# Softmax sums applied to the attention's values through diagonal tiles, in a hybrid encoder block on one core

## The chip, the core and the metric

The kernel runs on one core of one Trainium2 chip. The metric is the device time of one execution in microseconds (us). The engines are named as the profile names them: PE (TensorE, matrix products and transposes), PEld (its weight loads, which overlap its products), DVE (VectorE), ACT (ScalarE), POOL (GpSimd) and SP (SyncE, which here issues most of the DMAs). Each engine works through its own queue in order, and semaphores make it wait for the others.

## The reference

One encoder layer over 1024 tokens of width 1024, in float32. A combined projection of the normalised input feeds two groups of heads: attention in a window, with 8 query heads that share 2 key and value heads of width 64, and a gated DeltaNet (GDN) of 4 heads in both directions. Their outputs are concatenated, projected by W_out and added to the input; a feed-forward network with squared ReLU and a last normalisation follow. The change lies in the attention, for a block of 128 queries against a band of up to three blocks of keys:

```python
scores = jnp.einsum("bnqkgd,bnskd->bnkgqs", qb, kb).astype(jnp.float32) * (ATTN_HEAD_DIM ** -0.5)
scores = scores + bias
scores = jnp.where(valid, scores, -1e30)
probs = jax.nn.softmax(jnp.concatenate([scores, sink_col], axis=-1), axis=-1)[..., :-1]
out = jnp.einsum("bnkgqs,bnskd->bnqkgd", probs.astype(v.dtype), vb)
```

The softmax has one more column, a learned sink for each head, which enters its sum and has no value. So each query's output is a sum of values weighted by exponentials, divided by one number for each query and head.

## The kernel before, in words

The layer runs in stages: the norm and the transposes of the input, the projections, the preparation of the GDN (triangular inversions), the attention and the two scans of the GDN, the output projection, then the feed-forward network as products of a fast block scheme. The large products are made of three matmuls with operands split into a high and a low part (L124, L125, L126; L119 makes the high part on ACT, L120 the low part on POOL).

From about 335 to 590 us of the span two streams of work are woven together by weights: generators yield an estimate of the work that they issued, and the weaver takes the stream that is furthest behind. One stream is `output()`: the attention, then the attention's half of the output projection (`out_attn`), then the GDN's half (`out_all`, which calls `out_gdn` for each block of 128 tokens) with the tokens of the second half of the feed-forward input (`tokens_second`). The other has the last inversions and the scans forward and backward. This gives the order in which the program is written; a scheduler that runs over it then sets each engine's order.

The attention goes over 8 blocks of queries n and the 2 key heads kv. `attn_scores` makes the scores of 4 query heads (two matmuls each, L544 and L545), adds the bias and takes the maximum on DVE (L546), exponentiates on ACT with the sum as an accumulated output (L558), adds the sink's part to the sum and takes the reciprocal on DVE (L559, L560), and then multiplies the probabilities of each head by it, three heads on DVE and one on POOL (all recorded at L563). Three steps later `attn_transpose` turns the probabilities on PE (L573, four transposes for each block of keys) and ACT copies them out of PSUM (L575). When both key heads are there, `attn_value` multiplies them with the values (L585: for each block of keys a pair of matmuls, one for each key head, with 64 columns of weights each, so that the output has the two key heads in the two halves of the partitions and 4 heads x 128 queries in its columns); DVE copies the result (L588), and SP stores it (L589) in a buffer in HBM, `mad`. `query` loads the next queries by a DMA that POOL issues (L594).

`out_attn` loads a block of `mad` back (L885), splits it (L119, L120) and projects it, with DVE adding to the residual stream (L876). `out_gdn` sums squares on ACT (L900), makes the norm's factor in small operations on DVE (L902 to L905) and POOL (L906), multiplies by it on DVE (L907), transposes on PE (L910) and multiplies by the gate on DVE (L911). `tokens_second` transposes the normalised rows (L209), scales them on ACT (L966, L214), makes the low parts and differences on DVE (L215, L970), and splits the differences (L949 on ACT, L950 on DVE or POOL). The scans' matmuls are L797, and their steps on DVE L810, L815, L816, L825, L836 and L843. The inversions are the lines L720 to L764.

Matmul results lie in two rings of 4 PSUM buffers: `psA` (scores, transposed probabilities, values, output projection) and `psB` (scans, tokens). In SBUF there are rings of equal buffers, among them `pg` (28), `sc` (4), `wr` (4) and `pt` (12).

Of the kernel before, what the change touches and what calls it, by code (L numbers as in the profile page):

```python
# [16 lines left out]
P = 128  # L17
# [60 lines left out]
class Block:  # L78
# [198 lines left out]
    def proj_ab(self, raw):  # L277
# [5 lines left out]
        nc.vector.tensor_copy(out=whz[:, :, 0:16], in_=whl[:, :, 0:16].bitcast(F32))  # L283
        zero = self.small((P, NK * 16), bufs=1, tag="zab")
        nc.gpsimd.memset(zero, 0.0)
# [11 lines left out]
        for c in range(NT):  # L297
            nc.tensor.transpose(ps[:, c, :], ab[:, c * P:(c + 1) * P], self.ident[0:32, 0:32])
        abt = self.small((P, NT, 32), bufs=1, tag="abt")
        nc.vector.tensor_copy(out=abt, in_=ps)  # L300
# [3 lines left out]
    def gates(self, ps):  # L304
# [3 lines left out]
        mk = lambda name: c.tile([P, NT, 8], F32, name=name)  # L308
        tmp = lambda: self.small((P, NT, 8), bufs=6, tag="gt")
        vt = nc.vector  # L310
# [29 lines left out]
        nc.tensor.matmul(gps[:, 1], self.ones, g, start=True, stop=True)  # L340
        gc2 = self.small((P, NT, 8), bufs=1, tag="gc2")
        self.ngc, self.egc, self.negc, self.egl, self.ew = (mk(n) for n in ("ngc", "egc", "negc", "egl", "ew"))
# [10 lines left out]
        rr = self.sc((64, 2, P))  # L353
        part = self.small((64, 3, P), bufs=1, tag="gparts", dt=BF16)
        nc.scalar.copy(out=part[:, 0, :], in_=tp)
# [176 lines left out]
    def attn_scores(self, n, kv, mx, q, mk):  # L532
# [4 lines left out]
        for gp in range(2):  # L537
# [12 lines left out]
            tiles.append(s)  # L550
        nm, es, sm = (self.small((P, 4), tag="nm", bufs=12) for _ in range(3))
        ns = self.nsink[:, 4 * kv:4 * kv + 4]
# [7 lines left out]
        nc.vector.reciprocal(out=sm, in_=sm)  # L560
        for g in range(4):
            s = tiles[g // 2][:, g % 2, :width]
            (nc.gpsimd if g == 3 else nc.vector).tensor_scalar(out=s, in0=s, scalar1=sm[:, g:g + 1], scalar2=None,  # L563
                                                               op0=ALU.mult)
        return tiles, list(range(lo, hi))

# [11 lines left out]

    def attn_value(self, n, pts, kbs):
        nc = self.nc  # L580
        ps = self.ps("psA")
        last = len(kbs) - 1
        for j in range(last, -1, -1):
            for kv in (1, 0):
                nc.tensor.matmul(ps[64 * kv:64 * kv + 64, :], self.va[:, kbs[j], 64 * kv:64 * kv + 64],  # L585
                                 pts[kv][j].rearrange("p g q -> p (g q)"), start=j == last, stop=j == 0)
        o = self.pt()
        nc.vector.tensor_copy(out=o, in_=ps)  # L588
        nc.sync.dma_start(out=self.mad[n], in_=o)  # L589
# [7 lines left out]
    def attention(self):  # L597

        steps = [(n, kv) for n in range(NT) for kv in range(2)]
        qs = self.qs  # L600
        open_, pts = [], []

        def close():
            n, kv, tiles, kbs = open_.pop(0)
            pts.append(self.attn_transpose(tiles, kbs))
            yield 1.3
            if kv == 1:
                self.attn_value(n, pts[:], kbs)
                pts.clear()
                yield 2.6  # L610

        for i, (n, kv) in enumerate(steps):
            mk = self.pg if i % 3 == 2 else self.wr
            open_.append((n, kv, *self.attn_scores(n, kv, self.small((P, 4), tag="nm", bufs=12), qs.pop(0), mk)))
            if i + 2 < len(steps):
                qs.append(self.query(*steps[i + 2]))
            yield 1.3
            if len(open_) > 2:
                yield from close()
        while open_:  # L620
            yield from close()
# [756 lines left out]
```

## Time and profile before

| what | value |
|---|---|
| time, three runs | 1256.77, 1258.15, 1258.52 us; median 1258.15 |
| span of the profiled execution | 1253.3 us |
| its own time | not given |
| mean granted clock of TensorE | 0.983 |
| PE, PEld busy | 95%, 77% of the span |
| DVE, ACT, POOL busy | 68%, 50%, 46% |

The span goes from the first to the last instruction of one profiled execution; the time of a run has what lies around it too. A group's line in the profile gives the line of the code, the engine, the operation, output and inputs with their sizes, how many there were, the busy time of all and the mean of one in ns, and behind the second bar the engine's idle time just ahead of them with what ended it. An f32 matmul is recorded as two instructions. The ends of matmuls are modelled, so the busy time of PE says that it had work, not that it ran at its peak.

### The profile page before, as it was taken

How to read it: one execution, taken by the hardware profiler on the slowest of the kernel's cores; microseconds unless marked ns; L12 is line 12 of the kernel's file. 1: busy time of each engine (PE TensorE's matmuls, PEld its weight loads, DVE VectorE, ACT ScalarE, POOL GpSimd, SP SyncE). 2: the span in 40 equal slices, each digit the busy share in tenths (PEclk: the TensorE clock that was granted, in tenths of full speed). 3: DMA queues.
4: the chain of work that ended last, by engine and by line, in shares of the span. 5: the costliest groups of instructions: out<-in, count | busy, mean ns of one | idle time of the engine just before them, and what ended most of it. 6: DMA issues, size and time to landing. Idle time of an engine off the chain costs nothing.

```text
span 1253.3 us, 18527 instructions
## 1 busy us (share of the span) xinstructions
PE 1191.6 (95%) x6482; PEld 967.2 (77%) x6482; DVE 854.9 (68%) x1528; ACT 621.4 (50%) x1347; POOL 580.3 (46%) x488
## 2 busy tenths in 40 slices
PE   7999999899789989998999999999999999999997
PEld 5778777677568868877788888888777888888885
DVE  5667667982389986676655454544668797886976
ACT  6455688335485752125464554545545434444343
POOL 5354211362432433144573534535445665655595
PEclk9999999899889999998999999999999999999999
DMA  7134344441956678122234344443678624434323
GB/s 239 52 121 133 101 171 140 139 126 40 223 168 158 190 216 296 60 84 85 84 131 159 132 151 143 154 159 134 223 280 280 223 85 167 151 121 148 95 90 135
DMA packets 121630, 187.62 MB, mean 150 GB/s; under 512 B 11043, under 2 KB 64416, under 8 KB 121537
## 3 DMA queue, kind: packets, MB, share of 16 engines
q1 hardware_dynamic: 96708, 152.58, 37.9%
q10 hardware_dynamic: 16381, 29.67, 6.3%
q0 software_dynamic: 8448, 4.20, 1.9%
q8 instruction: 51, 0.84, 0.3%
q14 instruction: 42, 0.34, 0.1%
HBM read 122.39 MB, written 63.49 MB: 148 GB/s over the span
## 4 chain that ended last, share of the span: by engine, by line
PE 49%; DVE 6%; DMA 3%; issue 2%; POOL 1%; ACT 1%; ACTq 0%; POOLq 0%; DVEq 0%; SPq 0%
PE psA L124 8%; PE psA L125 8%; PE psA L126 8%; PE psB L126 7%; PE psB L125 7%; PE psB L124 7%; DMA pg<-sd 3%; PE psB L797 2%; DVE pg L1154 1%; DVE pt L1163 1%; DVE wr L1166 1%; PE psB L209 1%; DVE pg L1199 1%; DMA sd<-pt 0%; DVE wr L1161 0%
## 5 line engine op out<-in xcount | busy, mean ns | idle before, releaser
L124 PE MATMUL psA<-pg,wh 128*128 128x512 f32 x416 | 167.6, 404 | 2.1 <-ACT pt L458 2.1
L126 PE MATMUL psA<-pg,wl 128*128 128x512 f32 x416 | 166.9, 401 | 0.0
L125 PE MATMUL psA<-pg,wh 128*128 128x512 f32 x416 | 166.5, 400 | 0.0
L120 POOL TENSOR_TENSOR wl<-wr,wh 128x512 fp32r<-128x512 f32 x44 | 70.2, 1618 | 154.0 <-ACT wh L119 153.9
L1154 DVE TENSOR_TENSOR pg<-pg 128x512 fp32r<-128x512 f32 x112 | 122.7, 1127 | 18.8 <-ACT pg L1153 18.6
L120 POOL TENSOR_TENSOR wh<-wr,wh 128x512 fp32r<-128x512 f32 x32 | 47.9, 1518 | 131.5 <-ACT wh L119 131.5
L1071 ACT ACTIVATE pt<-pt 128x512 f32<-128x512 f32 x64 | 40.4, 632 | 122.7 <-DVE pt L1061 122.7
L125 PE MATMUL psA<-pg,pg 128*128 128x512 f32 x256 | 99.7, 391 | 0.5 <-POOL pg L120 0.5
L124 PE MATMUL psA<-pg,pg 128*128 128x512 f32 x256 | 99.0, 391 | 1.0 <-DVE pg L1199 1.0
L126 PE MATMUL psA<-pg,pg 128*128 128x512 f32 x256 | 99.7, 389 | 0.0
L120 POOL TENSOR_TENSOR pg<-wr,pg 128x512 fp32r<-128x512 f32 x48 | 73.4, 1560 | 51.0 <-ACT pg L119 51.0
L124 PEld LDWEIGHTS psA<-pg,wh 128*128 128x128 f32 x416 | 79.2, 190 | 21.3 <-ACT pt L458 2.4
L125 PEld LDWEIGHTS psA<-pg,wh 128*128 128x128 f32 x416 | 79.3, 191 | 19.7 <-issue 0.9
L126 PEld LDWEIGHTS psA<-pg,wl 128*128 128x128 f32 x416 | 79.1, 190 | 18.6
L1153 ACT CAST pg<-pg 128x512 fp32r<-128x512 f32 x112 | 67.2, 620 | 41.3 <-DMA pg<-sd 31.0
L126 PE MATMUL psB<-pg,pg 128*128 128x512 f32 x192 | 75.0, 390 | 1.3 <-DVE pg L1154 1.3
L125 PE MATMUL psB<-pg,pg 128*128 128x512 f32 x192 | 75.0, 391 | 0.8 <-POOL pg L120 0.7
L124 PE MATMUL psB<-pg,pg 128*128 128x512 f32 x192 | 74.7, 390 | 0.4 <-ACT pg L1153 0.4
L119 ACT CAST wh<-wr 128x512 fp32r<-128x512 f32 x76 | 43.6, 623 | 45.5 <-PE psA L125 24.8
L1061 DVE TENSOR_TENSOR pt<-psB,pt 128x512 f32<-128x512 f32 x39 | 26.9, 689 | 55.1 <-PE psB L126 30.1
L1061 DVE TENSOR_TENSOR pt<-psA,pt 128x512 f32<-128x512 f32 x39 | 26.8, 689 | 55.0 <-PE psA L126 39.5
L124 PEld LDWEIGHTS psA<-pg,pg 128*128 128x128 f32 x256 | 48.0, 188 | 12.6 <-DVE pg L1199 2.3
(385 smaller groups left out, 3307.7 us busy)
## 6 DMA issues: line engine op xcount, KB each, us to landing
sd<-pt ACTq DMA_DIRECT2D x112, 256.0 KB, 2.2
pg<-sd SPq DMA_DIRECT2D x112, 256.0 KB, 2.9
wr<-in_w_ffn_in SPq DMA_DIRECT2D x32, 512.0 KB, 3.8
wr<-in_w_in SPq DMA_DIRECT2D x22, 512.0 KB, 4.8
pg<-in_x SPq DMA_DIRECT2D x16, 512.0 KB, 5.4
wr<-in_w_ffn_out SPq DMA_DIRECT2D x16, 512.0 KB, 4.8
sc<-kvd SPq DMA_DIRECT2D x14, 512.0 KB, 4.1
kvd<-pt SPq DMA_DIRECT2D x16, 256.0 KB, 2.8
```

Source lines behind the costliest of these rows:

```text
L119: nc.scalar.copy(out=h, in_=raw)
L120: (eng or nc.gpsimd).tensor_tensor(out=l, in0=raw, in1=h.bitcast(F32), op=ALU.subtract)
L124: nc.tensor.matmul(ps, wh, xh, start=first, stop=False, skip_group_check=onto)
L125: nc.tensor.matmul(ps, wh, xl, start=False, stop=False, skip_group_check=onto)
L126: nc.tensor.matmul(ps, wl, xh, start=False, stop=last, skip_group_check=onto)
L209: self.nc.tensor.transpose(ps[:, i * P:(i + 1) * P], row[:, k * P:(k + 1) * P], self.ident)
L797: nc.tensor.matmul(ps[:, h - g.start, :], left(h), right[:, h, :], start=True, stop=True)
L1061: self.nc.vector.tensor_tensor(out=out, in0=in0, in1=in1, op=ALU.add)
L1071: self.nc.scalar.activation(out=c, in_=c, func=AF.Relu)
L1153: nc.scalar.copy(out=s[:, 0], in_=raw)
L1154: v.tensor_tensor(out=s[:, 1], in0=raw, in1=s[:, 0].bitcast(F32), op=ALU.subtract)
L1163: v.tensor_tensor(out=b["T2"], in0=b["B22"], in1=b["T1"], op=ALU.subtract)
```

## The change

The multiplication of the probabilities is taken out. `attn_scores` now returns the reciprocals of the sums as well, 128 queries x 4 heads. For each of the 16 pairs of query block and key head, POOL multiplies the identity by them (`diagonal`, recorded at the line after L567): a tile of four 128x128 diagonals. `attn_value` first multiplies a matrix of ones with 64 columns by each key head's diagonals: the sum over the partitions leaves one row with the reciprocal of each query and head, the same in all 64 output partitions, as the values' output has them. ACT copies that out of PSUM into the second diagonal's tile, and DVE multiplies the values by it where it copied them before.

```diff
-        for g in range(4):
-            s = tiles[g // 2][:, g % 2, :width]
-            (nc.gpsimd if g == 3 else nc.vector).tensor_scalar(out=s, in0=s, scalar1=sm[:, g:g + 1], scalar2=None,
-                                                               op0=ALU.mult)
-        return tiles, list(range(lo, hi))
+        return tiles, list(range(lo, hi)), sm
+
+    def diagonal(self, r):
+
+        dg = self.buf("dg", 2, (P, 4, P))
+        self.nc.gpsimd.tensor_tensor(out=dg, in0=self.ident.unsqueeze(1).to_broadcast([P, 4, P]),
+                                     in1=r.unsqueeze(2).to_broadcast([P, 4, P]), op=ALU.mult)
+        return dg
...
-    def attn_value(self, n, pts, kbs):
-        nc = self.nc
+    def attn_value(self, n, pts, kbs, dgs):
+
+        nc = self.nc
+        rec = self.ps("psA")
+        for kv in (1, 0):
+            nc.tensor.matmul(rec[64 * kv:64 * kv + 64, :], self.ones[:, 64 * kv:64 * kv + 64],
+                             dgs[kv].rearrange("p g q -> p (g q)"), start=True, stop=True)
+        scale = dgs[1].rearrange("p g q -> p (g q)")
+        nc.scalar.copy(out=scale, in_=rec)
         ps = self.ps("psA")
...
         o = self.pt()
-        nc.vector.tensor_copy(out=o, in_=ps)
+        nc.vector.tensor_tensor(out=o, in0=ps, in1=scale, op=ALU.mult)
         nc.sync.dma_start(out=self.mad[n], in_=o)
...
-            n, kv, tiles, kbs = open_.pop(0)
+            n, kv, tiles, kbs, r = open_.pop(0)
+            dgs.append(self.diagonal(r))
             pts.append(self.attn_transpose(tiles, kbs))
             yield 1.3
             if kv == 1:
-                self.attn_value(n, pts[:], kbs)
+                self.attn_value(n, pts[:], kbs, dgs[:])
                 pts.clear()
-                yield 2.6
+                dgs.clear()
+                yield 3.0
```

Besides, the ring of the small tiles of `attn_scores` grows from 12 to 16, and some small temporaries at the start of the kernel (L284, L299, L309, L341, L354) move into `pt` buffers, which makes room for the two diagonal tiles. In the lines of the changed kernel, L546 and L547 are the score matmuls, L578 the transposes of the probabilities, L580 their copy, L589 the new matmuls, L592 the new copy, L597 the value matmuls, L600 the new product, L811 the scans' matmuls; L876, L907, L910, L911, L950 and L970 have become L890, L921, L924, L925, L964 and L984.

The change moves instructions as well. On PE, in the middle of the attention before: the transposes of a block's probabilities, scan matmuls, then the value matmuls (an operand's number tells buffers apart, `x2` is two matmuls in a row).

```order
L573 MATMUL psA_4399<-ident,wr_4132 128x128 x2
L573 MATMUL psA_4399<-ident,wr_4141 128x128 x2
L797 MATMUL psB_4406<-sc_4324,sc_4323 128x128 x2
L797 MATMUL psB_4411<-sc_4324,sc_4323 128x128 x2
L797 MATMUL psB_4416<-sc_4198,pg_4319 128x128 x2
L797 MATMUL psB_4421<-sc_4324,pt_4326 128x128 x2
L585 MATMUL psA_4434<-pt_4404,pg_2381 64x512
L585 MATMUL psA_4434<-pt_4316,pg_2381 64x512
```

The same place on PE after:

```order
L578 MATMUL psA_4408<-ident,wr_4115 128x128 x2
L578 MATMUL psA_4408<-ident,wr_4124 128x128 x2
L811 MATMUL psB_4364<-sc_4284,sc_4283 128x128 x2
L811 MATMUL psB_4369<-sc_4284,sc_4283 128x128 x2
L811 MATMUL psB_4374<-sc_4156,pg_4279 128x128 x2
L589 MATMUL psA_4415<-dg_4392,ones 64x512
L589 MATMUL psA_4415<-dg_4308,ones 64x512
L811 MATMUL psB_4379<-sc_4284,pt_4286 128x128 x2
L597 MATMUL psA_4419<-pt_4413,pg_2374 64x512
L597 MATMUL psA_4419<-pt_4329,pg_2374 64x512
```

The new pair stands between the block's transposes and its value matmuls, here with scan matmuls on both sides; that is so for seven of the eight blocks.

At the end of the attention on PE, between the last value matmul and the first matmul of the output projection (L124), before:

```order
L585 MATMUL psA_4927<-pt_4888,pg_2381 64x512
L797 MATMUL psB_4919<-sc_4869,pt_4871 128x128 x2
L797 MATMUL psB_4923<-sc_4869,pt_4871 128x128 x2
L797 MATMUL psB_4947<-sc_4869,pg_4621 128x128 x2
...
L797 MATMUL psB_5050<-sc_4943,pg_4318 128x128 x2
L797 MATMUL psB_5055<-sc_4943,pg_4318 128x128 x2
L124 MATMUL psA_4975<-pg_4746,pt_4969 128x512
```

The same place on PE after:

```order
L597 MATMUL psA_4952<-pt_4891,pg_2374 64x512
L811 MATMUL psB_4975<-sc_4924,pt_4926 128x128 x2
L811 MATMUL psB_4979<-sc_4840,pg_4547 128x128 x2
L811 MATMUL psB_4984<-sc_4924,pt_4926 128x128 x2
...
L811 MATMUL psB_5068<-sc_5025,sc_5024 128x128 x2
L811 MATMUL psB_5073<-sc_4924,pg_4279 128x128 x2
L124 MATMUL psA_4996<-pg_4675,pt_4990 128x512
```

Before, 14 such rows, 28 scan matmuls, stand between the two; after, 10 rows, 20 matmuls.

On DVE, where the last `out_gdn` meets `tokens_second`, before:

```order
L215 SCALAR_TENSOR_TENSOR pg_6097<-psB_6092,cols,pg_6097 128x512
L905 TENSOR_TENSOR sm_5997<-sm_5997,sq_1234 128x4
L970 SCALAR_TENSOR_TENSOR pg_6085<-psB_6092,cols,pg_6085 128x512
L215 SCALAR_TENSOR_TENSOR pg_6136<-psB_6131,cols,pg_6136 128x512
L970 SCALAR_TENSOR_TENSOR pg_6124<-psB_6131,cols,pg_6124 128x512
L907 TENSOR_TENSOR wr_5995<-pg_3794,sm_5998 128x512
L950 TENSOR_TENSOR pg_6140<-pg_6085,pg_6140 128x512
L215 SCALAR_TENSOR_TENSOR pg_6169<-psB_6164,cols,pg_6169 128x512
L970 SCALAR_TENSOR_TENSOR pg_6143<-psB_6164,cols,pg_6143 128x512
L911 SCALAR_TENSOR_TENSOR wr_5994<-psA_6010,cols,wr_5995 128x512
```

The same place on DVE after:

```order
L984 SCALAR_TENSOR_TENSOR pg_6117<-psB_6124,cols,pg_6117 128x512
L917 TENSOR_SCALAR sm_5990<-sm_5990 128x4
L964 TENSOR_TENSOR pg_6133<-pg_6078,pg_6133 128x512
L918 RECIPROCAL sm_5990<-sm_5990 128x4
L215 SCALAR_TENSOR_TENSOR pg_6162<-psB_6157,cols,pg_6162 128x512
L984 SCALAR_TENSOR_TENSOR pg_6136<-psB_6157,cols,pg_6136 128x512
L919 TENSOR_TENSOR sm_5990<-sm_5990,sq_1227 128x4
L215 SCALAR_TENSOR_TENSOR pg_6190<-psB_6185,cols,pg_6190 128x512
L984 SCALAR_TENSOR_TENSOR pg_6169<-psB_6185,cols,pg_6169 128x512
L964 TENSOR_TENSOR pg_6194<-pg_6136,pg_6194 128x512
L921 TENSOR_TENSOR wr_5988<-pg_3775,sm_5991 128x512
L925 SCALAR_TENSOR_TENSOR wr_5987<-psA_6003,cols,wr_5988 128x512
```

The multiplication by the norm's factor (L907, now L921), which stood behind two of the four L215 and L970 pairs, stands behind all four and both L950 (L964). On PE the order there is as before: the 32 transposes of the tokens, the four transposes of this block (L910, now L924), the matmuls of the output projection.

More of the change, by code (lines that the diff above doesn't have):

```diff
@@ L283, in proj_ab @@
         nc.vector.tensor_copy(out=whz[:, :, 0:16], in_=whl[:, :, 0:16].bitcast(F32))
-        zero = self.small((P, NK * 16), bufs=1, tag="zab")
+        zero = self.pt((P, NK * 16))
         nc.gpsimd.memset(zero, 0.0)
@@ L298, in proj_ab @@
             nc.tensor.transpose(ps[:, c, :], ab[:, c * P:(c + 1) * P], self.ident[0:32, 0:32])
-        abt = self.small((P, NT, 32), bufs=1, tag="abt")
+        abt = self.pt((P, NT, 32))
         nc.vector.tensor_copy(out=abt, in_=ps)
@@ L308, in gates @@
         mk = lambda name: c.tile([P, NT, 8], F32, name=name)
-        tmp = lambda: self.small((P, NT, 8), bufs=6, tag="gt")
+        spare = self.pt((P, 8, NT, 8))
+        free = iter(range(8))
+        tmp = lambda: spare[:, next(free)]
         vt = nc.vector
@@ L340, in gates @@
         nc.tensor.matmul(gps[:, 1], self.ones, g, start=True, stop=True)
-        gc2 = self.small((P, NT, 8), bufs=1, tag="gc2")
+        gc2 = tmp()
         self.ngc, self.egc, self.negc, self.egl, self.ew = (mk(n) for n in ("ngc", "egc", "negc", "egl", "ew"))
@@ L353, in gates @@
         rr = self.sc((64, 2, P))
-        part = self.small((64, 3, P), bufs=1, tag="gparts", dt=BF16)
+        part = self.pt((64, 3, P), BF16)
         nc.scalar.copy(out=part[:, 0, :], in_=tp)
@@ L550, in attn_scores @@
             tiles.append(s)
-        nm, es, sm = (self.small((P, 4), tag="nm", bufs=12) for _ in range(3))
+        nm, es, sm = (self.small((P, 4), tag="nm", bufs=16) for _ in range(3))
         ns = self.nsink[:, 4 * kv:4 * kv + 4]
@@ L600, in attention @@
         qs = self.qs
-        open_, pts = [], []
+        open_, pts, dgs = [], [], []
         def close():
-            n, kv, tiles, kbs = open_.pop(0)
+            n, kv, tiles, kbs, r = open_.pop(0)
+            dgs.append(self.diagonal(r))
             pts.append(self.attn_transpose(tiles, kbs))
@@ L607, in close @@
             if kv == 1:
-                self.attn_value(n, pts[:], kbs)
+                self.attn_value(n, pts[:], kbs, dgs[:])
                 pts.clear()
-                yield 2.6
+                dgs.clear()
+                yield 3.0
         for i, (n, kv) in enumerate(steps):
             mk = self.pg if i % 3 == 2 else self.wr
-            open_.append((n, kv, *self.attn_scores(n, kv, self.small((P, 4), tag="nm", bufs=12), qs.pop(0), mk)))
+            open_.append((n, kv, *self.attn_scores(n, kv, self.small((P, 4), tag="nm", bufs=16), qs.pop(0), mk)))
             if i + 2 < len(steps):
```

## The prediction

> **What bounds the kernel now.** The first view is the page: the span and the busy time of each engine.
>
> ```profile
> span 1253.3 us, 18527 instructions
> PE 1191.6 (95%) x6482; PEld 967.2 (77%) x6482; DVE 854.9 (68%) x1528; ACT 621.4 (50%) x1347; POOL 580.3 (46%) x488
> ```
>
> PE is busy for 95% of the span, so as a whole the kernel is bound by TensorE. The change touches only the attention, so the second view cuts out its neighbourhood: the last inversion (335 to 365), the attention woven with the scans (to 475), the attention's half of the output projection woven with the last scan (to 530), and the end of that scan (to 545). The columns are the stretch, its length, the busy time of PE, of the weight loads (PEld), of DVE, ACT and POOL, then granted clock, DMA share and GB/s.
>
> ```profile
> 335.00:365.00 30.00, 23.21 (x451) 18.50 (x450) 21.73 (x70) 24.43 (x61) 14.45 (x18) 0.77 0.60 160
> 365.00:475.00 110.00, 101.53 (x771) 83.51 (x772) 101.32 (x337) 68.86 (x200) 35.06 (x31) 1.00 0.73 209
> 475.00:530.00 55.00, 55.00 (x305) 47.37 (x304) 32.84 (x90) 9.64 (x35) 15.17 (x13) 1.00 0.48 168
> 530.00:545.00 15.00, 12.15 (x71) 10.33 (x70) 13.89 (x34) 5.20 (x15) 8.46 (x6) 0.89 0.17 52
> ```
>
> The attention's stretch is the one place where two engines are near their limit together: PE 101.53 and DVE 101.32 of 110 us. Just behind it, from 475 on, PE has no idle time at all. Which of the two ends the other's waits is the third view, PE's waits from 335 to 475, with total, times and longest:
>
> ```profile
> PE psB L753 <- DVE pt L746: 3.1, 3, 2.2
> PE psB L720 <- DMA pg<-atd: 3.1, 2, 2.1
> PE psB L797 <- DVE sc L815: 2.8, 3, 1.2
> PE psA L573 <- DVE pt L588: 1.7, 1, 1.7
> PE psA L585 <- ACT pt L575: 1.6, 2, 0.9
> PE psA L544 <- DMA pt<-qad: 0.8, 1, 0.8
> PE psB L797 <- DVE sc L810: 0.6, 1, 0.6
> PE psB L761 <- ACT pt L755: 0.5, 1, 0.5
> PE psB L797 <- DVE sc L825: 0.5, 1, 0.5
> PE psA L544 <- DVE pt L588: 0.3, 1, 0.3
> ```
>
> They sum to 14.0 us: DVE ends 3.1 + 2.8 + 1.7 + 0.6 + 0.5 + 0.3 = 9.0, ACT 1.6 + 0.5 = 2.1, DMA 3.1 + 0.8 = 3.9. So in 140 us PE stands still for 14, and a lighter DVE can give back 9 of them at most. Against that, whatever is added to PE is paid in full, since PE works the rest of the time.
>
> **Removed: the 64 multiplications of the probabilities.** The groups of their line, from 335 to 475, with the busy time of DVE and of POOL:
>
> ```profile
> 335.00:475.00 140.00, 24.43 (x48) 20.93 (x16) 0.95 0.70 198
> ```
>
> DVE loses 24.43 us in 48 instructions, POOL 20.93 in 16. DVE is not on the end's path by itself; what comes back is a share of the 9.0 us. I estimate it from two sides. By proportion: DVE's share falls from (21.73 + 101.32) / 140 = 87.9% to (123.05 - 24.43) / 140 = 70.4%; at 59.7% (32.84 of 55, the next stretch) PE waits for nobody, so between these points 9.0 x (70.4 - 59.7) / (87.9 - 59.7) = 3.4 us stay and 5.6 go. If every wait that DVE ends is only its queue, all 9.0 go. I take the middle, -7.3. The bounds are -2.0 (only the two waits that the attention's own copy L588 ended, 1.7 + 0.3) and -11.1 (9.0 and the 2.1 behind ACT as well). The 3.9 behind DMA stay.
>
> **Added on PE: 16 matmuls of ones by diagonal tiles.** They have the form of the value matmuls (128x64 weights, 512 columns, f32), whose price is in PE's timeline (start, length, line, recorded count; two records are one f32 matmul):
>
> ```profile
> 408.42 2.80 PE L585 MATMUL psA<-pt,pg 128*64 128x512 f32 x12 [0.90 <-ACT pt L575]
> 411.15 0.44 PE L544 MATMUL psA<-pg,pt 128*128 128x384 f32 x1
> 463.21 1.94 PE L585 MATMUL psA<-pt,pg 128*64 128x512 f32 x8 [0.68 <-ACT pt L575]
> 465.08 1.16 PE L797 MATMUL psB<-sc,pt 128*128 128x128 f32 x8
> 466.07 2.32 PE L797 MATMUL psB<-sc,pg 128*128 128x128 f32 x16
> ```
>
> Three pairs take 411.15 - 408.42 = 2.73 us from their start to the next kind's, two pairs 465.08 - 463.21 = 1.87. So a further pair costs 0.86, and the block has 2.73 - 3 x 0.86 = 0.15 of its own. In the order of the changed program seven of the eight new pairs stand alone among matmuls with 128 columns of weights, and pay the 0.15 each; one stands right ahead of its value matmuls. That is 8 x 0.86 + 7 x 0.15 = +7.9; the bounds are 6.9 (no 0.15) and 8.1 (all eight alone). The Trainium skill, TensorEngine Tiling (Array Packing), Key Properties, says that a change of the tiling mode drains TensorE. The row agrees in kind, with 0.15 us for the way in and out; without such a rule the sum would be 1.0 us lower. I stay with the row.
>
> **Added elsewhere.** POOL's 16 products of the identity with a sum's column are 512 columns of TensorTensor, so like these:
>
> ```profile
> L865 POOL TENSOR_TENSOR pg<-pg,pg 128x512 fp32r<-128x512 f32 x4 | 6.0, 1511 | 14.9 <-ACT pg L863 14.9
> L865 POOL TENSOR_TENSOR wl<-pg,wh 128x512 fp32r<-128x512 f32 x3 | 3.9, 1289 | 8.3 <-ACT wh L863 8.2
> L575 ACT COPY pt<-psA 128x512 f32<-128x512 f32 x44 | 23.6, 585 | 18.7 <-PE psA L573 18.7
> L588 DVE COPY pt<-psA 128x512 f32<-128x512 f32 x8 | 5.5, 684 | 1.6 <-PE psA L585 1.5
> L1199 DVE TENSOR_TENSOR pg<-pg,psB 128x512 f32<-128x512 f32 x48 | 32.0, 678 | 21.2 <-PE psB L126 16.1 <-POOL pg L1202 5.0
> ```
>
> 16 x 1.29 to 1.51 is 20.6 to 24.2 us on POOL, for 20.93 that leave; the query loads that POOL issues stand between them as they stood between the multiplications, so 0. ACT gets 8 copies at 0.585, 4.7 us, covered by 110 - 68.86 = 41 idle us there; without that cover they would be a wait of the value matmuls, which is the third rival. On DVE the product with the scale (0.678, as L1199) replaces the copy (0.684): 0. The new waits: PE's pair waits for POOL's second diagonal, with the block's value matmuls behind it; the diagonals are issued ahead of the block's transposes, three steps after their sums, so POOL is ahead by the transposes at least. DVE's product waits for PE's values and ACT's copy, with scan steps behind it, as they stood behind the copy L588. POOL's next diagonal waits until that product has read the tile, with a query load behind it; POOL is busy for 35.06 of 110 us: 0 for each. The temporaries of the gates that move to other buffers, at the start, change no duration: 0, with 0.5 as the most.
>
> **Moved: the start of the output projection.** The last value block is followed by its DVE copy, a store, the load of the same rows, an ACT cast, and the first output matmul; PE has only scan matmuls for that time:
>
> ```profile
> 465.22 0.69 DVE L588 COPY pt<-psA 128x512 f32<-128x512 f32 x1 [0.34 <-PE psA L585]
> 472.79 0.62 ACT L119 CAST pt<-wr 128x512 fp32r<-128x512 f32 x1 [3.94 <-DMA wr<-mad]
> 473.46 0.50 PE L124 MATMUL psA<-pg,pt 128*128 128x512 f32 x1
> ```
>
> The chain takes 473.46 - 465.08 = 8.4 us and was just filled by 28 scan matmuls. In the new order 20 stand there; the other eight have been moved ahead of the value block. Eight at (466.07 - 465.08) / 4 = 0.25 are 2.0 us of filling that is missing. What ends first I can't tell, so +1.0, bounds 0 and 2.0.
>
> **Moved: the last gated DeltaNet block.** The new order changes a place far behind, too. There DVE's L907, the product ahead of PE's transposes L910, stood after two pairs of L215 and L970; now it stands after all four and both L950 of its engine, while PE still has L910 ahead of 48 projection matmuls:
>
> ```profile
> 588.73 0.68 DVE L907 TENSOR_TENSOR wr<-pg,sm 128x512 f32<-128x512 f32 x1
> 589.33 0.68 DVE L950 TENSOR_TENSOR pg<-pg,pg 128x512 fp32r<-128x512 f32 x1
> 589.93 0.74 DVE L215 SCALAR_TENSOR_TENSOR pg<-psB,cols,pg 128x512 fp32r<-128x512 f32 x1
> 590.59 0.74 DVE L970 SCALAR_TENSOR_TENSOR pg<-psB,cols,pg 128x512 f32<-128x512 f32 x1
> 593.23 1.34 DVE L950 TENSOR_TENSOR pg<-pg,pg 128x512 fp32r<-128x512 f32 x1
> 590.06 0.69 ACT L214 ACTIVATE pg<-psB,cols 128x512 fp32r<-128x512 f32 x1
> 589.46 0.66 PE L910 MATMUL psA<-ident,wr 128*128 128x128 f32 x4
> ```
>
> Two more pairs are 2 x (590.59 - 589.93) x 2 = 2.64, two L950 at 589.93 - 589.33 are 1.20: L907 begins 3.8 us later, at 592.6, and L910 at 593.3. The fourth pair's input, L214, is done at 590.75 and does not hold it up. PE has nothing else queued ahead: +3.8. Bounds: 3.0, when the small operations of L902 to L905 fill gaps that they did not fill before; 4.6, when one L950 takes 1.34 in place of its 0.60.
>
> **The sum.** -7.3 + 7.9 + 1.0 + 3.8 = +5.4 us: span 1258.7. The own time of the profiled execution is not given; the median of the runs, 1258.15, is 4.9 above its span, so I set the sum against the median: 1263.6. With all bounds at their best -11.1 + 6.9 + 0 + 3.0 = -1.2, at their worst -2.0 + 8.1 + 2.0 + 4.6 = +12.7: 1257.0 to 1270.9 for this case. A difference of 0.2%, 2.5 us, is about what a measurement of this kernel can tell from none.
>
> **Rivals.** First, faster: DVE sets the whole stretch, and PE's busy time hides slack. PE's weight loads are 83.51 of 110 us there, 75.9%; from 475 on, where PE waits for nothing, they are 47.37 of 55, 86.1%. At that density the attention's PE work would take 83.51 / 0.861 = 97.0 us, which leaves 13.0. If DVE's 24.43 us free all of it, and the 3.1 us behind L746 go too: 7.9 - 13.0 - 3.1 + 3.8 = -4.4, 1253.8. It decides as soon as more than 11 us come back. For it: DVE is at 92% there. Against it: only 9.0 us of waits name DVE, and the short matmuls (transposes of 128 columns, 384-column scores) may simply pack worse. The Trainium skill, Trainium Kernel Development and Optimization, Best Practices, has the rule behind it: distance to the limit is judged by the share of weight loads, not by busy matmuls. Chance 0.18.
>
> Second, no difference: the late L907 costs nothing, since PE waits anyway at the next step, when the second half's tokens become ready. Then -7.3 + 7.9 + 1.0 = +1.6, 1259.8. For it: that part of the program waits on a chain of DVE. Against it: 48 projection matmuls stand ready behind L910. Chance 0.22.
>
> Third, slower still: the sums' PSUM buffer is one more of the four that scores, transposes and values share, and it is free only when ACT has copied it. ACT's copy can stand behind the next block's exponentials:
>
> ```profile
> L558 ACT ACTIVATE wr<-wr,nm 128x384 f32<-128x384 f32 x32 | 19.4, 612 | 4.2 <-DVE nm L553 4.2
> ```
>
> One such wait of 0.61 in each of eight blocks is +4.9: +10.3, 1268.5. It decides from about one exponential per block on. Against it: ACT is idle 37% there, and in the order the copy follows directly on the transposes' copies in most blocks. Chance 0.10.
>
> That the change doesn't do what it says is excluded: in the changed program's order all 48 multiplications on DVE are gone.
>
> **How the numbers follow.** The forecast has 0.50, so slower by over 0.2% has 0.50 + 0.10 = 0.60, within 0.2% 0.22, faster 0.18. The range goes down to 1254.5, close to the first rival's 1253.8, which leaves out some 0.12, and up to 1270.0, just under the forecast's own upper bound, which leaves out some 0.06.
>
> **What would show it.** The profile after should have PE's busy time up by 8 us and DVE's down by 24; in the attention's stretch waits of PE behind DVE at 1 to 4 us in place of 9.0; the new pairs at 0.86 to 1.01 us each; a gap of about 3.8 us on PE ahead of the last transposes L910; and waits for the sums' copy of under 1 us together. The forecast is wrong if the stretch from 365 to 475 gets shorter than 110 us by several us (the first rival), if PE goes through the last block without the gap (the second), or if the rows of waits name the new copy eight times (the third).

## The result and the profile after

The changed kernel takes 1274.03 us (median of 4 runs, 1273.12 to 1276.48) against 1258.34 before (4 runs), 15.7 us slower. The ratio on record is 1.0132, interval 1.0116 to 1.0149, which is 16.6 us. The forecast was 5.4 us slower, in a range that ended at 1270.0. The sign held, the size did not: three of its four terms were too kind to the change, each for its own reason, and the fourth, the new matmuls, was too hard on it.

The page of the changed kernel, span and busy times:

```profile
span 1272.6 us, 18548 instructions
PE 1206.3 (95%) x6514; PEld 973.4 (76%) x6514; DVE 827.4 (65%) x1480; ACT 625.1 (49%) x1355; POOL 576.0 (45%) x488
```

DVE does 27.5 us less, as intended. PE does 14.7 us more, where the new matmuls account for 8. The fair comparison is by the same work, not by the clock: the stretch from the first score matmul to the last value matmul. Its ends are 335.97 and 464.55 us before (columns as in the prediction's windows):

```profile
335.97:464.55 128.58, 113.81 (x1152) 92.93 (x1151) 113.52 (x376) 88.63 (x244) 45.10 (x45) 0.95 0.68 188
```

and 337.70 and 479.13 after:

```profile
337.70:479.13 141.43, 128.77 (x1221) 99.82 (x1219) 99.09 (x349) 95.00 (x261) 45.72 (x47) 0.94 0.64 180
```

The stretch is 12.85 us longer, and PE has 69 records more in it. The new matmuls are 32 of these; 36 others are 18 scan matmuls (two records each) that the new order has put ahead of the last value block: 174 stand there where 156 stood. PE's idle time is 12.7 us (141.43 - 128.77) where it was 14.8.

Scan matmuls that moved ahead are missing behind, so a longer piece gives the net loss: from the first score to the first of the tokens' transposes (L209, at 582.97 before and 595.72 after) PE has the same matmul records in both kernels, but for the 32 new ones. It took 247.0 us and takes 258.0, 11.0 more. The next piece, from there to the first matmul behind the output projection, has the same records too (one more in the first row is the next matmul); it takes 6.3 us more:

```profile
582.97:606.69 23.72, 23.72 (x109) 20.33 (x110) 14.59 (x24) 10.48 (x19) 7.54 (x9) 0.88 0.26 89
595.72:625.77 30.05, 25.77 (x108) 21.90 (x109) 13.82 (x24) 10.64 (x21) 7.19 (x9) 0.80 0.21 71
```

From there to the end it is 646.6 us before and 646.8 after. So the loss lies in two places: the attention with the start of the output projection, where the prediction's terms came to +1.6, and the last block, where it had +3.8.

The first number to check is the price of a pair. PE's timeline after has one at 380:

```profile
380.44 1.08 PE L589 MATMUL psA<-dg,ones 128*64 128x512 f32 x4
381.45 1.16 PE L811 MATMUL psB<-sc,sc 128*128 128x128 f32 x8
```

381.45 - 380.44 is 1.01 us, to the hundredth the price read from the value blocks before. What PE waits for from 335 to 500 us, the five largest:

```profile
PE psB L767 <- DVE pt L760: 3.3, 2, 2.7
PE psB L734 <- DMA pg<-atd: 2.9, 2, 1.6
PE psB L811 <- DMA pt<-pd: 2.8, 1, 2.8
PE psA L124 <- ACT pt L119: 2.7, 1, 2.7
PE psA L546 <- DVE nm L548: 1.3, 2, 0.7
```

L767 is the wait of the inversion (L753 before), which the change doesn't touch. The waits behind DVE in the attention proper did shrink, from 5.9 us to 2.3. Two waits are new, one behind a load of the scan (`pd`) and one behind the ACT cast that the output projection starts with. Both are in PE's timeline:

```profile
466.22 1.16 PE L811 MATMUL psB<-sc,pt 128*128 128x128 f32 x8 [2.83 <-DMA pt<-pd]
...
488.17 0.65 PE L124 MATMUL psA<-pg,pt 128*128 128x512 f32 x1 [2.72 <-ACT pt L119]
488.62 0.63 PE L125 MATMUL psA<-pg,pt 128*128 128x512 f32 x1
489.05 0.63 PE L124 MATMUL psA<-pg,pt 128*128 128x512 f32 x1
```

Behind the second gap the projection's matmuls start 0.43 us apart (489.05 - 488.62). The same thing shows at the last gated DeltaNet block. There are DVE's late product, PE's four transposes behind it, and the projection matmuls behind those:

```profile
595.72 6.27 PE L209 MATMUL psB<-ident,pg 128*128 128x128 f32 x32 [3.58 <-DVE pg L205]
606.27 1.11 PE L924 MATMUL psA<-ident,wr 128*128 128x128 f32 x4 [4.28 <-DVE wr L921]
607.04 0.78 PE L124 MATMUL psA<-pg,pt 128*128 128x512 f32 x1
...
611.03 0.50 PE L124 MATMUL psA<-pg,pt 128*128 128x512 f32 x1
...
613.22 0.40 PE L124 MATMUL psA<-pg,pt 128*128 128x512 f32 x1
613.46 0.40 PE L125 MATMUL psA<-pg,pt 128*128 128x512 f32 x1
```

From the first of the 32 transposes to L924 it is now 10.55 us. Before, the 32 transposes began at 582.97:

```profile
582.97 6.51 PE L209 MATMUL psB<-ident,pg 128*128 128x128 f32 x32 [3.59 <-DVE pg L205]
```

That made 589.46 - 582.97 = 6.49 us to L910. The difference is the slip, 4.1 us, which the prediction had at 3.8. But the nine matmuls from 607.04 to 611.03 take 0.44 each, where 0.24 is the pace from 613 on. The granted clock in these windows says why:

```profile
606.00:608.00 2.00, 1.73 (x6) 1.58 (x7) 0.79 (x2) 0.00 (x0) 1.34 (x1) 0.50 0.00 0
608.00:610.00 2.00, 2.00 (x6) 1.57 (x5) 0.18 (x1) 0.62 (x1) 1.09 (x1) 0.50 0.21 45
612.00:614.00 2.00, 2.00 (x10) 1.60 (x10) 0.69 (x1) 0.00 (x0) 0.00 (x0) 1.00 0.69 225
```

PE stood idle, its clock was halved, and the work behind the gap paid for that with another 9 x (0.44 - 0.24) = 1.8 us, and the four transposes with 0.4 (0.77 us to the next matmul against 0.41 at full pace, in the run e5 below). So by these rows a gap of 4 us cost 4.1 + 1.8 + 0.4 = 6.3, all of what this piece has lost. The prediction counted only the idle time.

### The profile page after: what moved, and what is told of

Read it like the earlier page. It is cut to its first block, busy times and chain, and to the rows that moved or that the text cites. A ratio compares the mean times of both kernels' runs of the same rounds, so it can differ in the third digit from the quotient of the medians.

```text
span 1272.6 us, 18548 instructions
## 1 busy us (share of the span) xinstructions
PE 1206.3 (95%) x6514; PEld 973.4 (76%) x6514; DVE 827.4 (65%) x1480; ACT 625.1 (49%) x1355; POOL 576.0 (45%) x488
## 4 chain that ended last, share of the span: by engine, by line
PE 59%; DVE 9%; issue 5%; ACT 4%; POOL 4%; DMA 3%; SPq 1%; POOLq 0%; DVEq 0%; ACTq 0%
PE psA L124 10%; PE psA L125 10%; PE psA L126 10%; PE psB L125 7%; PE psB L124 7%; PE psB L126 7%; PE psB L811 4%; PE psA L597 1%; POOL pg L120 1%; PE psA L578 1%; DVE pt L1177 1%; PE psA L546 1%; SPq L502 1%; DMA pg<-in_w_out 1%; DMA pg<-sd 1%
## 5 line engine op out<-in xcount | busy, mean ns | idle before, releaser
L124 PE MATMUL psA<-pg,wh 128*128 128x512 f32 x416 | 167.9, 404 | 1.7 <-ACT pt L460 1.7
L124 PE MATMUL psA<-pg,pg 128*128 128x512 f32 x256 | 99.0, 391 | 1.4 <-DVE pg L1213 0.9
L124 PEld LDWEIGHTS psA<-pg,wh 128*128 128x128 f32 x416 | 79.6, 191 | 21.0 <-ACT pt L460 2.1
L124 PE MATMUL psB<-pg,pg 128*128 128x512 f32 x192 | 74.6, 389 | 0.0
L124 PEld LDWEIGHTS psA<-pg,pg 128*128 128x128 f32 x256 | 48.0, 188 | 13.1 <-DVE pg L1213 2.1
```

The costliest lines, as they stand in the source:

```text
L124: nc.tensor.matmul(ps, wh, xh, start=first, stop=False, skip_group_check=onto)
```

## Theories and experiments

Theory A, formed from these views: the loss is a sum of order effects (a start of the output projection that is not filled, and the late block, each with slow matmuls behind its gap) on top of paid pairs, against a relief of DVE that gives back little. The rivals were that the additions are hidden and the relief is large, and that PE would wait in those places anyway. The runs, with the kernel before on the same chip:

| run | what it is | us (median) | ratio to before, 95% interval |
|---|---|---|---|
| e1_relief | before, multiplications taken out (not normalised) | 1255.01 | 0.9975 [0.9961, 0.9989] |
| e2_add | changed, multiplications put back (normalised twice) | 1279.36 | 1.0156 [1.0134, 1.0178] |
| e4_temps | before, with the moved temporaries | 1258.41 | 1.0003 [0.9990, 1.0017] |
| e8_fold | changed, factor inside the transposes | 1280.66 | 1.0172 [1.0150, 1.0195] |
| e3_tail | changed, yield 2.6 | 1268.29 | 1.0092 [1.0071, 1.0114] |
| e5_slip | changed, short norm factor | 1267.57 | 1.0089 [1.0062, 1.0115] |
| e6_both | e3 and e5 together | 1262.97 | 1.0046 [1.0029, 1.0063] |
| e10_fill | changed, gap filled with spare transposes | 1273.85 | 1.0127 [1.0105, 1.0149] |
| e12_nopairs | e6 without the pairs (wrong factors) | 1259.08 | 1.0016 [1.0003, 1.0028] |
| e11_row | e6, factors by transposes | 1252.72 | 0.9974 [0.9961, 0.9987] |
| e7_before_short | before, short norm factor | 1259.89 | 1.0019 [1.0007, 1.0032] |

The kernel before took 1258.48, 1256.93 and 1256.91 us beside the first four rows, the next four and the last three, so what is compared below are ratios, one percent of which is 12.6 us. A difference between two rows has the intervals of both in it: by an estimate from them, 3.0 to 3.9 us to either side against the changed kernel, and 2.7 for e12 and e11 against e6.

**e1_relief: the relief alone.**

```diff
-        for g in range(4):
-            s = tiles[g // 2][:, g % 2, :width]
-            (nc.gpsimd if g == 3 else nc.vector).tensor_scalar(out=s, in0=s, scalar1=sm[:, g:g + 1], scalar2=None,
-                                                               op0=ALU.mult)
```

> The kernel before without the 64 multiplications of the probabilities and with nothing in their place, so the attention's output is not normalised. The order on PE and DVE at the start of the output projection and at the last gated DeltaNet block is that of before. Theory A (what DVE's relief gives back is a few of the waits that DVE ended in the attention, as the changed profile shows: 5.9 us outside the inversions before, 2.3 after): 3 to 6 us faster than before, 1252 to 1255 us. Theory B (the relief is worth the 13 us of slack that the weight loads suggest, and the cost of the additions is hidden in the changed kernel's sum): 10 us faster or more, under 1249. Theory C (DVE's relief gives nothing, other waits take its place): within 1.5 us of before.

It is 3.1 us faster than before (0.25%; 1.4 to 4.9 us by the interval), at the lower end of A. From its first score to its last value matmul, and its four largest waits of PE from 335 to 475 us:

```profile
337.97:463.26 125.29, 115.24 (x1153) 92.84 (x1151) 88.89 (x328) 87.97 (x244) 22.90 (x27) 0.95 0.68 188
```

```profile
PE psB L726 <- ACT pt L719: 2.7, 1, 2.7
PE psA L581 <- ACT pt L571: 2.6, 3, 1.1
PE psB L749 <- DVE pt L742: 2.0, 1, 2.0
PE psB L793 <- DVE sc L811: 0.9, 1, 0.9
```

DVE's share of the stretch falls from 88% to 71%, and the stretch gets 3.3 us shorter. The waits behind DVE come to 3.6 us (two more rows have 0.4 and 0.3) where they were 9.0. The value matmuls (L581 here) wait for ACT's copies of the transposed probabilities (L571), and a step of the inversion (L726) for ACT as well: 5.3 us behind ACT where 2.1 were. But such sums vary from profile to profile: e4 and e7, which have the attention of before, show 7.4 and 8.1 behind DVE, and 4.7 and 3.4 behind ACT. So 3.8 to 5.4 us of waits behind DVE went, and that ACT took over a part of them is not shown.

**e2_add: the additions alone.**

```diff
         nc.vector.reciprocal(out=sm, in_=sm)
+        for g in range(4):
+            s = tiles[g // 2][:, g % 2, :width]
+            (nc.gpsimd if g == 3 else nc.vector).tensor_scalar(out=s, in0=s, scalar1=sm[:, g:g + 1], scalar2=None,
+                                                               op0=ALU.mult)
         return tiles, list(range(lo, hi)), sm
```

> The changed kernel with the 64 multiplications put back, so the normalisation is applied twice: all additions, no relief. The two moved places have the changed order. Theory A: the changed kernel plus what the relief gave, 1277 to 1280 us; PE's new pairs at 0.9 to 1.0 us each as before. Theory B: 1284 or more. Theory C: as the changed kernel, 1272.5 to 1275.5.

The ratio goes from 1.0132 to 1.0156: 3.0 us for the same multiplications from the other side. By itself this can't be told from nothing, but it is what e1 has: the relief is worth some 3 us.

**e4_temps: the moved temporaries.** The edits of L284, L299, L309, L341 and L354 and the ring of 16, on the kernel before.

> The kernel before with the moved temporaries and the larger ring of small tiles alone. In the profiles the changed kernel was 1.7 us late already at its first scores, ahead of every new instruction. If the moved temporaries do that: 1.5 to 2 us slower than before, about 1260, with the same steps at 285 and 320 us. If it is the clock's varying dips from execution to execution: no difference beyond 0.7 us.

No difference (1.0003). In its profile the first score is later by even 3.7 us than in that of before, yet the time is the same, so where a profiled execution stands at that point varies by itself. That settles the 1.7 us by which the changed kernel's first score came later (337.70 against 335.97). Its stretch from the first score to the last value matmul is 130.85 us, too, where before had 128.58: 2 us between the stretches of two single profiles prove nothing.

**e3_tail: the start of the output projection.**

```diff
-                yield 3.0
+                yield 2.6
```

> The changed kernel with one number changed, the estimate of work that the value step yields to the weaver (2.6 as before the change, where the change has 3.0). This puts 28 scan matmuls back between the last value matmul and the first output projection, as in the kernel before; all arithmetic is that of the changed kernel. Theory A (missing fill costs its idle 2.9 us and about 1.4 more at the half clock behind it): 4 us faster than the changed kernel, 1269 to 1271. Theory B (the load chain is waited for elsewhere anyway): 1273 to 1275.

The gain is 0.40%, 5.0 us (1.6 to 8.4 by the two intervals). The stretch, and the place where the gap was:

```profile
338.56:470.46 131.90, 124.27 (x1184) 96.04 (x1183) 90.32 (x327) 91.60 (x252) 40.21 (x44) 0.94 0.67 183
```

```profile
478.59 1.29 PE L811 MATMUL psB<-sc,pg 128*128 128x128 f32 x8
479.64 0.48 PE L124 MATMUL psA<-pg,pt 128*128 128x512 f32 x1
479.96 0.39 PE L125 MATMUL psA<-pg,pt 128*128 128x512 f32 x1
480.19 0.40 PE L124 MATMUL psA<-pg,pt 128*128 128x512 f32 x1
```

The output projection follows the scan matmuls without a gap and at full pace. The stretch has 37 records fewer than in the changed kernel, since the 18 scan matmuls are behind it again, and is 9.5 us shorter; the load of `pd` is no longer waited for either. Some of it was only moved: up to the first output projection the changed kernel had ten scan matmuls more than before (194 against 184), and these it does not have to do later. From the first score to the tokens' first transpose, which has the moved work on both sides, it is 250.6 us in place of 258.0: 7.4 less. So a number that looks like bookkeeping (an estimate of work, raised by 0.4 since the step does more) was worth some 5 us, about a third of the loss.

**e5_slip: the late block.** The norm's factor is sqrt(s2 / (q s2 / 128 + eps)), with q the sum of squares; with eps / s2 kept as a constant it is (q / 128 + eps / s2) to the power -1/2:

```diff
-        s2 = self.sq2[:, :, c]
-        nc.vector.tensor_tensor(out=so, in0=so, in1=s2, op=ALU.mult)
-        nc.vector.tensor_scalar(out=so, in0=so, scalar1=1.0 / P, scalar2=EPS, op0=ALU.mult, op1=ALU.add)
-        nc.vector.reciprocal(out=so, in_=so)
-        nc.vector.tensor_tensor(out=so, in0=so, in1=s2, op=ALU.mult)
-        nc.gpsimd.tensor_tensor(out=f, in0=so, in1=self.half_exp[:, 0:4], op=ALU.pow)
+        nc.vector.scalar_tensor_tensor(out=so, in0=so, scalar=1.0 / P, in1=self.eq2[:, :, c], op0=ALU.mult, op1=ALU.add)
+        nc.gpsimd.tensor_tensor(out=f, in0=so, in1=self.nhalf_exp[:, 0:4], op=ALU.pow)
...
```

> The changed kernel with the norm's factor of the gated DeltaNet blocks made by one small DVE operation and POOL's power in place of four and the power (the same value, with a constant worked out beforehand), which brings the last block's product back behind two of the four pairs, as in the kernel before. The fill at the start of the output projection stays short. Theory A (the late block costs 4.1 us of idle PE and 2.2 us of half clock behind it): 6 us faster than the changed kernel, 1267 to 1269. Theory B (only the idle time): 1269.5 to 1270.5. Theory C (PE would wait later anyway): 1273 to 1275.

The gain is 0.43%, 5.4 us, with 3.9 to either side, so the times alone don't tell the idle time (4.1) from the whole cost (6.3). In its timeline the last block's transposes (L920 here) wait 0.73 us in place of 4.28, and the projection runs at full pace behind them:

```profile
605.38 0.66 PE L920 MATMUL psA<-ident,wr 128*128 128x128 f32 x4 [0.73 <-DVE wr L917]
605.79 0.47 PE L124 MATMUL psA<-pg,pt 128*128 128x512 f32 x1
606.10 0.39 PE L125 MATMUL psA<-pg,pt 128*128 128x512 f32 x1
606.33 0.39 PE L126 MATMUL psA<-pg,pt 128*128 128x512 f32 x1
```

The piece from the tokens' first transpose to the end of the projection tells them apart:

```profile
598.28:622.60 24.32, 23.59 (x108) 20.19 (x109) 14.08 (x21) 10.65 (x21) 7.51 (x9) 0.89 0.25 87
```

It is 5.7 us shorter than in the changed kernel. It is also steady where whole times are not: 30.06 in e2 and 30.23 in e3, which have the late block, 23.71 in e4, 24.32 in e6. This profiled execution was the slowest of the six (1273.83 us, where they range from 1262.53), so its total shows none of the gain.

**e7_before_short: its control.** The same edit on the kernel before.

> Control: the kernel before with the short norm's factor alone, as the two repaired kernels have it. In the kernel before the last block's product stands behind two of the four pairs already, so nothing of the late block is there to repair: within 1.5 us of before. If it is faster by 3 us or more, part of what the repair of the late block gained is the shorter factor itself, and not the place.

It is slower than before by 0.19% (0.07 to 0.32), so the shorter factor is no gain in itself: it gained by the place that it brought about. No difference beyond 1.5 us was expected; why it costs 2.4 us stays open. In its profile the part behind the output projection, which the edit doesn't touch, takes 650.0 us in place of 646.6.

**e6_both: the two repairs together.** e3 and e5.

> Both repairs together on the changed kernel: the yield 2.6 with 30 scan matmuls of filling, and the short factor with the last product behind two pairs. Theory A: the two gains add, 10 us faster than the changed kernel, 1262.5 to 1265.5; what is left against before is then pairs 8.0 less relief 3.5. Theory B: 1268 or more, since one gap closed opens another.

The ratio is 1.0046: 0.86% less than the changed kernel, 10.8 us, against 5.0 and 5.4 for the two alone. Within 3 us they add. Two thirds of the loss were order, not arithmetic.

**e10_fill: the slow clock by itself.**

```diff
+            if k == 3:
+                spare = self.ps("psB")
+                for i in range(24):
+                    self.transpose_row(b12, i % 4, spare, i % 4)
             yield 0.5
```

> The changed kernel with 24 transposes more, of a tile that nothing needs, into a PSUM buffer that nothing reads, right ahead of the last block's four transposes on PE: they fill most of the 4.3 us gap there and change no other engine's order. Theory A (the gap lowers the granted clock to half for some 4 us behind it): the last block's transposes start where they did, and the projection matmuls behind them run at 0.23 us in place of 0.43; 2 us faster than the changed kernel, about 1272, though more work is done. Theory B (the slow matmuls behind the gap have another cause): 1274 or slower by up to 1 us.

PE's timeline there, with the 24 spare transposes, the last block's transposes and the projection:

```profile
603.08 2.84 PE L209 MATMUL psB<-ident,pg 128*128 128x128 f32 x24 [1.01 <-ACT pg L980]
606.38 0.66 PE L924 MATMUL psA<-ident,wr 128*128 128x128 f32 x4 [0.46 <-DVE wr L921]
606.79 0.47 PE L124 MATMUL psA<-pg,pt 128*128 128x512 f32 x1
607.11 0.39 PE L125 MATMUL psA<-pg,pt 128*128 128x512 f32 x1
607.34 0.39 PE L126 MATMUL psA<-pg,pt 128*128 128x512 f32 x1
```

The block's transposes start where they did (606.38 against 606.27), and the matmuls behind run at 0.23 us at once: with the gap filled the slow matmuls are gone, as in e5, where the gap is short: it was their cause, as far as one profile of each can show it. The time is nevertheless that of the changed kernel (1.0127 against 1.0132). In the profile the kernel came out of the projection 2.2 us ahead (623.61 against 625.77), and then met slow matmuls at 643, which left 0.6 of it, and at 977 us, where the changed kernel's execution had none; that one had some at 932 us, where this one had none. And 2 us are less than the 3.5 that these runs can tell. So the mechanism is shown at its place, and its gain in the total is not.

**e8_fold: the factor inside the transposes.**

```diff
-                nc.tensor.transpose(ps[:, g, :], tiles[g // 2][:, g % 2, j * P:(j + 1) * P], self.ident)
+                nc.tensor.matmul(ps[:, g, :], tiles[g // 2][:, g % 2, j * P:(j + 1) * P], dg[:, g, :], start=True, stop=True)
...
```

The pairs, their copies and the product are left out as well, and the yield is 2.6 again, as in e3.

> The changed kernel with the normalisation put into the transposes: each transpose of probabilities becomes an ordinary matmul with the diagonal tile in place of the identity, so the 16 matmuls with ones, the 8 ACT copies and the products are gone, and DVE copies the values as before. Order at the start of the output projection: 30 scan matmuls of filling; at the last gated DeltaNet block the late order of the changed kernel. Theory A (cost by parts: pairs 8.0, missing fill with the slow clock behind it about 4, late block about 6, relief minus 3 to 6): about 12 us faster than the changed kernel, 1258 to 1264, near the kernel before. Rival (the transposes as ordinary f32 matmuls take longer than transposes, 0.25 against 0.11 us for 176 of them): 1274 or more.

The rival won: 1.0172, slower than the changed kernel. The transposes' groups of the kernel before:

```profile
L573 PE MATMUL psA<-ident,wr 128*128 128x128 f32 x120 | 16.8, 283 | 1.7 <-DVE pt L588 1.7
L573 PE MATMUL psA<-ident,pg 128*128 128x128 f32 x56 | 7.1, 276 | 0.0
```

and of this one:

```profile
L578 PE MATMUL psA<-dg,wr 128*128 128x128 f32 x240 | 31.3, 286 | 0.0
L578 PE MATMUL psA<-dg,pg 128*128 128x128 f32 x112 | 13.9, 276 | 0.0
```

176 transposes are 176 records, but 176 ordinary f32 matmuls of the same size are 352: 45.2 us busy in place of 23.9. The 21 us outweigh what is saved, the pairs (8 us of busy time) and the 5 of e3.

**e12_nopairs: what the pairs cost where they stand.**

```diff
-        rec = self.ps("psA")
-        for kv in (1, 0):
-            nc.tensor.matmul(rec[64 * kv:64 * kv + 64, :], self.ones[:, 64 * kv:64 * kv + 64],
-                             dgs[kv].rearrange("p g q -> p (g q)"), start=True, stop=True)
         scale = dgs[1].rearrange("p g q -> p (g q)")
-        nc.scalar.copy(out=scale, in_=rec)
...
```

> The kernel with both repairs, without the 16 matmuls with ones and without ACT's 8 copies: DVE multiplies the values by the diagonal tile itself, so the output is wrong by that factor; POOL's diagonals and DVE's product stay. Order at the two moved places as in the repaired kernel. Theory A (PE's added pairs are paid in full, 7 x 1.01 + 0.91 = 8.0 us, and the relief gives 3.5): 8 us faster than with them, 1.9 to 3.5 us faster than before, about 1254 to 1256. Theory B (PE has room for them, so the repaired kernel's remaining cost is elsewhere): 1260 or more.

Between the two theories: 1.0016 against 1.0046 with the pairs, 3.8 us for the pairs and ACT's eight copies of them. First its stretch and its largest wait behind ACT, of PE from 335 to 475 us (L592 are the value matmuls here), then the stretch of e6_both:

```profile
337.72:465.55 127.83, 116.14 (x1152) 93.44 (x1151) 92.52 (x328) 88.14 (x244) 40.50 (x44) 0.95 0.66 185
```

```profile
PE psA L592 <- ACT pt L580: 3.7, 4, 1.5
```

```profile
337.36:469.23 131.87, 123.58 (x1185) 95.58 (x1183) 90.68 (x327) 91.64 (x252) 40.51 (x44) 0.94 0.67 184
```

With the pairs PE is busy for 7.4 us more and the stretch is 4.0 us longer. Without them the value matmuls wait 3.7 us for ACT's copies of the transposes, and with them not at all. A pair stands just there, between the transposes and the value matmuls, so half of it lies in a wait that would be there otherwise.

**e11_row: a cheaper row.** POOL spreads the factors of both key heads over 64 columns each, and four transposes turn the tile:

```diff
-        rec = self.ps("psA")
-        for kv in (1, 0):
-            nc.tensor.matmul(rec[64 * kv:64 * kv + 64, :], self.ones[:, 64 * kv:64 * kv + 64],
-                             dgs[kv].rearrange("p g q -> p (g q)"), start=True, stop=True)
-        scale = dgs[1].rearrange("p g q -> p (g q)")
-        nc.scalar.copy(out=scale, in_=rec)
+        rec = self.ps("psA", (P, 4, P))
+        for g in range(4):
+            nc.tensor.transpose(rec[:, g, :], ex[:, g].rearrange("p v d -> p (v d)"), self.ident)
+        scale = ex.rearrange("p g v d -> p (g v d)")
+        nc.scalar.copy(out=scale, in_=rec.rearrange("p g q -> p (g q)"))
...
+            self.ex = self.buf("dg", 2, (P, 4, 2, 64))
+        self.nc.gpsimd.tensor_copy(out=self.ex[:, :, kv], in_=r.unsqueeze(2).to_broadcast([P, 4, 64]))
...
```

> The kernel with both repairs, with the row of factors made in another way: POOL spreads each factor over 64 columns, and four transposes of 128 columns for each block of queries turn that into the factors of both key heads, in place of two f32 matmuls with 512 columns. Theory A (PE's time is what counts, and a transpose of 128 columns takes 0.11 us against 1.01 for a pair): 8 x (1.0 - 0.45) = 4.4 us faster than the repaired kernel, 1258 to 1260, within 0.2% of before. Theory B (what counts is the wait for the factors, not PE's time): as the repaired kernel, 1262 to 1264.

It is the fastest that gives the normalised output, 0.9974 [0.9961, 0.9987]: 3.3 us faster than before, 9 us faster than e6_both, where A expected 4.4. Its stretch, and the group of its transposes:

```profile
336.06:464.48 128.42, 118.91 (x1184) 97.31 (x1183) 90.14 (x327) 92.14 (x252) 30.18 (x44) 0.93 0.67 187
```

```profile
L589 PE MATMUL psA<-ident,dg 128*128 128x128 f32 x32 | 4.8, 273 | 0.0
```

The stretch is 3.4 us shorter than in e6_both, near the 4.4 expected. More came unasked: in the order of this kernel the last block's product stands ahead of all four pairs, and from the tokens' first transpose to the last block's it is 3.2 us less. That is not all gained, since only 20 of the 32 transposes stand ahead of it there; the other 12 take 1.2 us behind the projection. Both gains together, less what is lost between them, are 5.6 us from the first score to the first matmul into `psB` behind the projection (287.5 against 293.1). It is the order again, this time on the right side, so the 9 us are not the price of the cheaper row; what the rest of them is stays open.

## Why the prediction was wrong, step by step

The arithmetic, relief and pairs, was forecast at +0.6 together and measures +0.9 (e1, and e12 against e6). That the sum held was luck: each of the two was put 4 us too high, and the errors cancel. The miss lies in the two moved places: +4.8 forecast, 10.8 measured (e6). Of the signs that were named, the pairs' price and the gap at the last block came; PE's busy time went up by 14.7 us, not 8. One slip of adding changes nothing: the ten waits come to 15.0 us, not 14.0.

- **The pairs** (+7.9): each costs what was read, 7 x 1.01 + 0.91 = 8.0. What failed is "whatever is added to PE is paid in full": with both repairs they lengthen the stretch by 4.0 and the time by 3.8 (e12 against e6), since half of each lies where the value matmuls would wait for ACT: 1.6 to 3.7 us in the profiles of before, e1, e4, e7 and e12, none in those of e3 and e6.
- **The relief** (-7.3): it measures -3.1 (e1) and -3.0 (e2). The line drawn between DVE's share and PE's waits came near: it said that 5.6 us of them go, and 3.8 to 5.4 went (e1 against before, e4 and e7). The step that failed is the middle between that and all 9.0: waits behind DVE of 3.6 us stayed at the lower load, and the time gained is no more than what went.
- **The start of the output projection** (+1.0, bounds 0 and 2.0): it measures 5.0 (e3; 1.6 to 8.4), and 7.4 in the profiles, above its bounds. This is the step that failed most. The chain of store, load and cast was the bound, as one of its two readings had it, so the fill that was missing showed as 2.7 us of wait. But the step counted only the matmuls missing behind the value block, not the 18 that now stood ahead of it in a stretch where PE has little slack, nor the scan load waited for there, nor the half clock behind the gap. No run separates these three.
- **The late block** (+3.8, bounds 3.0 and 4.6): as idle time right, 4.1. As a cost it measures 5.4 in the time (e5) and 6.3 in its piece of the profile, since the transposes and matmuls behind it ran at a granted clock of 0.50 up to some 611 us.
- **POOL at nothing**: right in the changed kernel, where no wait of PE names POOL, and even cheaper than the rows suggested, 1.035 us each in place of 1.29 to 1.51:

```profile
L568 POOL TENSOR_TENSOR dg<-ident,nm 128x512 f32<-128x512 f32 x16 | 16.6, 1035 | 70.6 <-PE psA L589 44.8 <-DVE pt L600 14.2 <-DVE nm L562 4.5
```

Of the rivals, none came true: the faster one had PE's slack freed by DVE, and e1 excludes that for the 13 us; the second had the late block free, and the gap and e5's piece exclude it; the third had waits for ACT's new copy, and the waits of the changed kernel name none.

What stays open: e6_both is 5.8 us above before. Relief (-3.1), pairs (+4.0) and the short factor as e7 measured it (+2.4) make 3.3. The remaining 2.5 are within these intervals, and no run tells what they are.

## What to carry to other kernels

Where an order is made by estimates and a scheduler, a change has two prices, its arithmetic and the order that it brings about; here the second was two thirds, and could be bought back with one estimate and four small instructions. An engine's relief was worth a third of the waits that named it, so ask how many of them stay at the lower load, and read them in more than one profile. What is added to a busy engine costs less where that engine would have waited. And a gap on PE of a few us is to be counted with the matmuls behind it, which may run at half clock.

## What was not expected of the hardware

After PE had stood idle for 2.7 and 4.3 us, the granted clock was 0.5 and 512-column matmuls were 0.43 us apart in place of 0.23, for some 4 us; in the profile with the second gap filled by transposes (e10) that was gone. Behind the 2.83 us wait at 466 us, though, the granted clock stayed at 1.00. The Trainium skill, TensorE: Matmul & The Clock Gate, Part 1, says that the hardware watches PE's activity in free-running windows of about 3.4 us, and halves the clock after an idle one. The trace agrees in the halving, with 0.50 in the windows above. It differs in the length: the wait of 2.72 us is shorter than such a window and was followed by the half clock all the same, that of 2.83 was not, and no run here tells why.

A transpose of a 128x128 f32 tile is one record and 0.10 us (four from 605.38 to 605.79 are 0.41), an f32 matmul of the same size two (e8, 45.2 us busy in place of 23.9): here, moving arithmetic into the transposes doubled their price.
